# Eight instead of six row blocks under the seven-product scheme, with two of its weight sums made by adding DMAs

## The chip, the cores and the metric

The kernel runs on one core of a Trainium2 chip. A core has five engines with instruction queues of their own: TensorE (PE: matmuls; PEld is its weight load), VectorE (DVE), ScalarE (ACT), GpSimd (POOL) and SyncE (SP), which here only issues DMAs. Sixteen DMA engines move data between the memory (HBM) and the on-chip buffer (SBUF). Matmuls write to PSUM banks. The metric is the device time of one execution, in microseconds; lower is better.

## The reference

A trunk of two layers on 256 tokens of width 2048. Each layer is a token mixer (attention in layer 0, a convolution module in layer 1), an MLP with a squared ReLU, and a gated embedding. All is in float32. The change lies in the MLPs:

```python
def sq_relu_mlp(hn, w1, w2):          # w1: 2048 x 8192, w2: 8192 x 2048
    a = jax.nn.relu(hn @ w1)
    return (a * a) @ w2

for i in range(DEPTH):                # DEPTH = 2
    hn = rmsnorm(h, norm_mix_g[i])
    h = h + (dsa_mixer(...) if i % 2 == 0 else conformer_conv(...))
    h = h + sq_relu_mlp(rmsnorm(h, norm_mlp_g[i]), mlp_w1[i], mlp_w2[i])
    h = h + jax.nn.sigmoid(h @ ple_w_gate[i]) * (p[i] @ ple_w_proj[i])
return rmsnorm(h, final_g)
```

## The kernel before

**Products of float32 numbers.** The 256 tokens are two token blocks of 128 (t). A weight matrix is read in *blocks* of 128 rows by 512 columns (256 KB). TensorE multiplies rounded numbers (float32r), so each operand is split into a rounded high part and the low rest, and each product of blocks is three matmuls: high by high, high by low, low by high. `halves` (lines 295 to 300) splits weights: ScalarE writes `wh` (L298), then VectorE writes `wl` = raw - wh (L299).

**Groups.** Weights are loaded, split and multiplied in groups of up to KG = 3 blocks: one DMA from SP's queue into one of RAWS = 6 `raw` buffers, one ScalarE and one VectorE instruction into one of SPLITS = 4 pairs of buffers `wh`, `wl`. This holds for all weight products of the kernel (`groups` serves `gemm_part` too). In most of the convolution module's first product the `wl` of a group is made by GpSimd.

**pair_gemm.** Each MLP runs in 4 blocks of 2048 hidden columns; a block is two `pair_gemm` calls on w1 and two on w2, so 32 calls in all (*pairs* below). A pair multiplies all 16 row blocks by two column blocks (n = 0, 1) for both t, into four PSUM banks named y, z, v, x. 16 row blocks by 2 by 2 are 64 products. For the first 2 * SP = 6 row blocks a scheme in the manner of Strassen is used: they are SP = 3 couples of an even and an odd row block, and the four weight blocks of a couple are a (even, n=0), b (even, n=1), c (odd, n=0), d (odd, n=1). Seven products with weights a, c, a+b, a+d+b, d, b+d and a+b+d+c take the place of eight (the code makes b+d before it adds it to a). `seven` makes one of the seven for all couples, `plain` the products of the other row blocks. The token side's sums are made once by the class `Sums` (`put`, lines 184 to 199: five small VectorE operations and two splits for a couple, against one split for two ordinary row blocks), and are used by all the pairs that read them.

**Sums of weights.** `add` (L246) adds one `raw` buffer to another on VectorE, 3 blocks at a time: four adds in a pair.

**Partial results.** Some banks are read before they are complete (x1, z1, x2, x3): `taken` reads a bank by ScalarE (L726, on w1) or by VectorE (L760, on w2), and later products write on in that bank, so the first of them waits for the read. Deferred work (`defer`) is written out at the next `step()` calls.

**Order.** The kernel is written in Tile: a scheduler orders each engine's instructions by priority and by its own estimate of time; on the chip every engine then works its queue in that order and waits by semaphores. A load waits until its `raw` buffer is free, a split until its `wh`/`wl` buffers are free, that is, until TensorE has finished the group that had them.

Of the kernel before, what the change touches and what calls it, by code (L numbers as in the profile page):

```python
# [13 lines left out]
ALU = mybir.AluOpType  # L14
# [6 lines left out]
TT = 2  # L21
KT = 16
NB = 512
KG = 3
D_FF = 8192
HD = 128
N_HEADS = 16
# [22 lines left out]
POOL_PW2 = 10  # L50
STATS_LAG = 14
POOL_FROM = 1
SP = 3
HELD = 8
RAWS = 6
SPLITS = 4


@with_exitstack
def encoder(ctx: ExitStack, tc: tile.TileContext, A, inv_freq, out):  # L60
    nc = tc.nc
# [10 lines left out]
    def mm_tile():  # L72
        return ps_mm.tile([P, NB], F32, name="pm", tag="mm")
# [33 lines left out]
    def step():  # L107
        due = [it for it in later if it[0] <= 0]
        later[:] = [it for it in later if it[0] > 0]
        for it in later:  # L110
            it[0] -= 1
        for it in due:
            it[1]()
# [48 lines left out]
    class Sums:  # L162
# [3 lines left out]
        def __init__(self, which, pool):  # L166
            self.main, self.more = [], []
            for p in "hl":
                self.main.append(acts.tile([P, KT, S], F32R, name="x" + p + which, tag="x" + p + which)
                                 .rearrange("p k s -> p (k s)"))  # L170
                self.more.append(pool.tile([P, 3, SP, P], F32R, name="s" + p + which, tag="s" + p + which))
            n = 4 * SP * P
            self.four = [v[:, :n].rearrange("p (m i f) -> p m i f", m=4, i=SP) for v in self.main]
            self.rest = [v[:, n:].rearrange("p (k s) -> p k s", s=S) for v in self.main]
# [37 lines left out]
    def pair_gemm(x, src, taken, first=False):  # L212


        bank = {"x": at_tile(), "y": mm_tile(), "v": mm_tile(), "z": mm_tile()}
        begun, again, left = set(), set(), {"x": 3 * SP, "y": SP, "v": SP, "z": 2 * SP}
        for v in left:
            left[v] += KT - 2 * SP
            left[v] *= 3

        def load(ks, n):
            raw = raw_tile(len(ks))
            nc.sync.dma_start(raw, src[:, ks.start:ks.stop:ks.step, n * NB:(n + 1) * NB])
            return raw

        def product(v, a, b, w, last=False):

            for j, (l, r) in enumerate(((a, w[0]), (a, w[1]), (b, w[0]))):
                left[v] -= 1
                nc.tensor.matmul(bank[v], l, r, start=v not in begun, stop=bool(left[v] == 0 or (last and j == 2)),  # L230
                                 skip_group_check=v in again)
                begun.add(v)
            if left[v] == 0:
                defer(0, lambda: taken(v, bank[v]))
            elif last:
                again.add(v)

        raws = {}

        def raw(name):  # L240
            if name not in raws:
                raws[name] = load(range(name in "cd", 2 * SP, 2), int(name in "bd"))
            return raws[name]

        def add(name, other):
            nc.vector.tensor_tensor(raw(name), raw(name), raw(other), op=ALU.add)  # L246

        def seven(m, v, name, plus=None, part=None):
            step()
            if plus:  # L250
                raw(name), raw(plus)
                add(name, plus)
            w = halves(raw(name))
            for i in range(SP):
                product(v, x.sums(0, m, i), x.sums(1, m, i), (w[0][:, i], w[1][:, i]), part is not None and i == SP - 1)
            if part:
                defer(0, lambda: taken(part, bank[v]))

        def plain(n, ks):
            step()  # L260
            w = halves(load(ks, n))
            for t, v in enumerate("zx" if n else "yv"):
                if t == 1 and len(ks) > 2:
                    step()
                for i, k in enumerate(ks):
                    product(v, x.block(0, k, t), x.block(1, k, t), (w[0][:, i], w[1][:, i]))

        ks = groups(2 * SP, KT - 2 * SP)
        raw("a")
        seven(0, "x", "a", part="x1")  # L270
        seven(5, "y", "c")
        plain(0, ks[0])
        seven(3, "z", "a", "b", part="z1")
        plain(0, ks[1])
        raw("d")
        seven(1, "x", "a", "d", part="x2")
        for r in ks[2:]:
            plain(0, r)
        seven(4, "z", "d")
        seven(2, "x", "b", "d", part="x3")  # L280
        plain_n2 = list(ks)
        seven(6, "v", "a", "c")
        for r in plain_n2:
            plain(1, r)

    def groups(k0, kn):

        n = -(-kn // KG)
        ends = [k0 + kn * i // n for i in range(n + 1)]
        return [range(i, j) for i, j in zip(ends, ends[1:])]  # L290

    def raw_tile(nk, n=NB):
        return wpool.tile([P, KG, NB], F32, name="raw", tag="raw", bufs=RAWS)[:, :nk, :n]

    def halves(r, low=None):

        wh, wl = (wpool.tile([P, KG, NB], F32R, name=v, tag=v, bufs=SPLITS)[:, :r.shape[1], :r.shape[2]] for v in ("wh", "wl"))
        recent[0] = nc.scalar.activation(wh, r, AF.Copy).ins  # L298
        (low or nc.vector).tensor_tensor(wl, r, wh.bitcast(F32), op=ALU.subtract)  # L299
        return wh, wl  # L300
# [539 lines left out]
    with tc.tile_pool(name="cnv", bufs=1) as cnv:  # L840
# [93 lines left out]
        for c, tiles in enumerate(PW_TILES):  # L934
            plan(c)
            n, n0 = len(tiles) * P, tiles[0] * P
# [141 lines left out]
```

## Time and profile before

| | us |
|---|---|
| median of 3 runs | 2275.61 (2275.28 to 2276.20) |
| the profiled execution | 2273.53 |
| its span, first to last instruction | 2271.8 |
| TensorE busy | 2253.1 (99%) |
| VectorE busy | 1783.6 (79%) |
| ScalarE busy | 1298.4 (57%) |
| GpSimd busy | 248.5 (11%) |
| DMA queue of SP | 57% of 16 engines |

The MLPs lie at about 395 to 1050 us and 1480 to 2140 us. One block of an MLP (four pairs) takes 169.73 us, five times alike. Busy shares are means over stages; how long an engine waited, and for whom, stands in the waits.

### The profile page before, as it was taken

Reading aid. Unit: us, or ns where it says so; the run is one execution under the profiler, and the core shown is the slowest. Engines: PE = TensorE matmul, PEld = TensorE weight load, DVE = VectorE, ACT = ScalarE, POOL = GpSimd, SP = SyncE. Lnnn points to the kernel's source line nnn. Section 1 sums busy time; section 2 is a strip of 40 time slices with the busy share of each in tenths; the row PEclk is TensorE's granted clock in tenths of the full one; section 3 lists DMA queues with packets and bytes.
Section 4 is the critical chain, followed back from the end, with each engine's and each line's share of the span. In section 5 each row is a group of like instructions: output and inputs, shape, how many; then the busy total and the mean of one; then the engine's idle time right before and its main releaser. Section 6 shows DMA issues by size and latency. Waiting matters only on the chain.

```text
span 2271.8 us, 27693 instructions
## 1 busy us (share of the span) xinstructions
PE 2253.1 (99%) x10510; PEld 1873.6 (82%) x10510; DVE 1783.6 (79%) x2075; ACT 1298.4 (57%) x1530; POOL 248.5 (11%) x150
## 2 busy tenths in 40 slices
PE   9999999999999999999999999999999999999998
PEld 7888878888888888888898887888888888888886
DVE  5658657888888888887558998788888888888854
ACT  6445546755755755754554644566566566466453
POOL 0112200000000000000038873100000000000001
PEclk9999999999999999999999999999999999999999
DMA  7655445655655655656647552656656656656653
GB/s 267 195 156 172 144 144 161 210 181 190 225 181 190 224 183 191 226 179 201 200 132 222 184 172 83 190 158 211 224 166 209 218 170 209 213 175 217 224 191 102
DMA packets 244869, 425.53 MB, mean 187 GB/s; under 512 B 11636, under 2 KB 57604, under 8 KB 244608
## 3 DMA queue, kind: packets, MB, share of 16 engines
q1 hardware_dynamic: 241872, 419.62, 57.0%
q10 hardware_dynamic: 2864, 4.15, 0.6%
q8 instruction: 82, 1.34, 0.3%
q14 instruction: 51, 0.42, 0.1%
HBM read 421.63 MB, written 2.10 MB: 187 GB/s over the span
## 4 chain that ended last, share of the span: by engine, by line
PE 98%; ACT 0%; DMA 0%; issue 0%; DVE 0%; POOL 0%; SPq 0%; POOLq 0%; DVEq 0%; ACTq 0%
PE pm L230 40%; PE at L230 18%; PE pm L323 11%; PE pm L325 11%; PE pm L324 11%; PE pt L745 1%; PE pm L880 1%; PE pt L404 1%; PE at L591 0%; PE at L638 0%; PE at L668 0%; DMA raw<-in_a_w_in 0%; PE pt L528 0%; PE at L323 0%; PE at L324 0%
## 5 line engine op out<-in xcount | busy, mean ns | idle before, releaser
L298 ACT ACTIVATE wh<-raw 128x1536 fp32r<-128x1536 f32 (+4 forms) x710 | 942.8, 1335 | 757.5 <-PE at L230 255.4
L299 DVE TENSOR_TENSOR wl<-raw,wh 128x1536 fp32r<-128x1536 f32 (+2 forms) x652 | 1033.7, 1598 | 356.8 <-ACT wh L298 354.2
L246 DVE TENSOR_TENSOR raw<-raw 128x1536 f32<-128x1536 f32 x128 | 224.6, 1754 | 19.0 <-DMA raw<-in_mlp_w 18.0
L323 PE MATMUL pm<-wh,xhA 128*128 128x512 f32 (+2 forms) x608 | 234.1, 388 | 1.4 <-ACT xhA L999 1.2
L324 PE MATMUL pm<-wl,xhA 128*128 128x512 f32 (+2 forms) x608 | 233.8, 385 | 0.0
L325 PE MATMUL pm<-wh,xlA 128*128 128x512 f32 (+2 forms) x608 | 231.8, 385 | 0.5 <-DVE xlA L1000 0.4
L324 PE MATMUL pm<-wl,xhB 128*128 128x512 f32 (+1 forms) x576 | 212.4, 369 | 0.0
L325 PE MATMUL pm<-wh,xlB 128*128 128x512 f32 (+1 forms) x576 | 211.5, 368 | 0.0
L323 PE MATMUL pm<-wh,xhB 128*128 128x512 f32 (+1 forms) x576 | 210.7, 369 | 0.4 <-ACT xhB L355 0.4
L230 PE MATMUL pm<-wl,xhB 128*128 128x512 f32 x528 | 206.6, 391 | 0.0
L230 PE MATMUL pm<-wl,xhA 128*128 128x512 f32 x528 | 206.4, 391 | 0.0
L230 PE MATMUL pm<-wh,xlA 128*128 128x512 f32 x528 | 206.2, 391 | 0.0
L230 PE MATMUL pm<-wh,xlB 128*128 128x512 f32 x528 | 206.2, 390 | 0.0
L230 PE MATMUL pm<-wh,xhA 128*128 128x512 f32 x528 | 197.4, 392 | 0.0
L230 PE MATMUL pm<-wh,xhB 128*128 128x512 f32 x528 | 197.2, 391 | 0.0
L909 DVE SCALAR_TENSOR_TENSOR at<-u,wdw,at 128x256 f32<-128x256 f32 x402 | 160.3, 484 | 0.0
L299 POOL TENSOR_TENSOR wl<-raw,wh 128x1536 fp32r<-128x1536 f32 (+3 forms) x58 | 154.4, 2670 | 34.6 <-ACT wh L298 32.6
L323 PEld LDWEIGHTS pm<-wh,xhA 128*128 128x128 f32 x608 | 114.4, 188 | 22.7 <-ACT xhA L999 1.5
L324 PEld LDWEIGHTS pm<-wl,xhA 128*128 128x128 f32 x608 | 114.4, 188 | 21.8 <-DVE wl L299 1.1
L325 PEld LDWEIGHTS pm<-wh,xlA 128*128 128x128 f32 x608 | 114.1, 188 | 22.1 <-DVE xlA L1000 1.4
L323 PEld LDWEIGHTS pm<-wh,xhB 128*128 128x128 f32 x576 | 108.5, 189 | 17.9 <-ACT xhB L355 0.6
L325 PEld LDWEIGHTS pm<-wh,xlB 128*128 128x128 f32 x576 | 108.6, 189 | 17.4 <-issue 0.2
(214 smaller groups left out, 3571.7 us busy)
## 6 DMA issues: line engine op xcount, KB each, us to landing
raw<-in_mlp_w SPq DMA_DIRECT2D x256, 768.0 KB, 6.1
raw<-in_mlp_w SPq DMA_DIRECT2D x128, 512.0 KB, 4.5
raw<-in_a_w_in SPq DMA_DIRECT2D x36, 768.0 KB, 4.3
raw<-in_ple_w_gate SPq DMA_DIRECT2D x32, 768.0 KB, 4.8
raw<-in_b_w_pw SPq DMA_DIRECT2D x48, 384.0 KB, 4.3
raw<-in_a_w_out SPq DMA_DIRECT2D x16, 768.0 KB, 4.5
raw<-in_b_w_pw SPq DMA_DIRECT2D x16, 768.0 KB, 4.4
raw<-in_a_w_in SPq DMA_DIRECT2D x18, 512.0 KB, 3.5
```

Of the source, the lines that this page charges most:

```text
L230: nc.tensor.matmul(bank[v], l, r, start=v not in begun, stop=bool(left[v] == 0 or (last and j == 2)), skip_group_check=v in again)
L246: nc.vector.tensor_tensor(raw(name), raw(name), raw(other), op=ALU.add)
L298: recent[0] = nc.scalar.activation(wh, r, AF.Copy).ins
L299: (low or nc.vector).tensor_tensor(wl, r, wh.bitcast(F32), op=ALU.subtract)
L323: nc.tensor.matmul(pm[t][:, :n], a, wh[:, i], start=k + i == 0, stop=False)
L324: nc.tensor.matmul(pm[t][:, :n], a, wl[:, i], start=False, stop=False)
L325: nc.tensor.matmul(pm[t][:, :n], b, wh[:, i], start=False, stop=k + i == kt - 1)
L404: nc.tensor.transpose(pt[:, k, t, :], h[:, t, (kk + k) * P:(kk + k + 1) * P], ident)
L745: nc.tensor.transpose(pt[:, k, t, :], both[t][:, 2 * j + k, :], ident)
L880: nc.tensor.matmul(acc, d.sets[0][0][:, i, :], u[:, kk, i:i + S], start=i == 0, stop=i == CONV_W - 1)
L909: nc.vector.scalar_tensor_tensor(dst, src, w, z, op0=ALU.mult, op1=ALU.add)
```

## The change

- SP goes from 3 to 4: the scheme covers 8 of 16 row blocks. KG goes from 3 to 2, so a group is two blocks everywhere in the kernel; RAWS goes from 6 to 9 and SPLITS from 4 to 6, which is the same room in SBUF.
- The four couples are two groups (`sets`), so each of the seven products is two splits of two blocks.
- The sums a+b and b+d are no longer made by VectorE from a loaded b: GpSimd issues a DMA that reads b from memory and adds it to the `raw` buffer that holds a (or d). b is never loaded to a buffer of its own, but read twice. The sums with d and c stay on VectorE.
- The order of the products is another, and GpSimd's scratch for DMA descriptors is 2048 instead of 1024.

```diff
-KG = 3
+KG = 2
-SP = 3
+SP = 4
-RAWS = 6
-SPLITS = 4
+RAWS = 9
+SPLITS = 6
...
+        sets = groups(0, SP)
         raws = {}
...
+        def rows(name, q):
+            return range(2 * q.start + (name in "cd"), 2 * q.stop, 2), int(name in "bd")
...
         def add(name, other):
-            nc.vector.tensor_tensor(raw(name), raw(name), raw(other), op=ALU.add)
...
+            for q in sets:
+                r = raw(name, q)
+                if other == "b":
+                    nc.gpsimd.dma_start(r, piece(*rows(other, q)), accum_op=ALU.add)
+                else:
+                    nc.vector.tensor_tensor(r, r, raw(other, q), op=ALU.add)
...
+        def seven(m, v, name, part=None):
+            for q in sets:
+                step()
+                w = halves(raw(name, q))
+                for j, i in enumerate(q):
+                    product(v, x.sums(0, m, i), x.sums(1, m, i), (w[0][:, j], w[1][:, j]), part and i == SP - 1)
...
         ks = groups(2 * SP, KT - 2 * SP)
-        raw("a")
         seven(0, "x", "a", part="x1")
+        add("a", "b")
         seven(5, "y", "c")
-        plain(0, ks[0])
-        seven(3, "z", "a", "b", part="z1")
-        plain(0, ks[1])
-        raw("d")
-        seven(1, "x", "a", "d", part="x2")
-        for r in ks[2:]:
+        for r in ks[:-2]:
             plain(0, r)
+        seven(3, "z", "a", part="z1")
+        add("a", "d")
         seven(4, "z", "d")
-        seven(2, "x", "b", "d", part="x3")
-        plain_n2 = list(ks)
-        seven(6, "v", "a", "c")
-        for r in plain_n2:
+        add("d", "b")
+        seven(1, "x", "a", part="x2")
+        add("a", "c")
+        plain(0, ks[-2])
+        seven(6, "v", "a")
+        seven(2, "x", "d", part="x3")
+        plain(0, ks[-1])
+        for r in ks:
             plain(1, r)
```

What the scheduler makes of it, at three places. On GpSimd, at the two ends of the first MLP, before (the held row belongs to the attention, the memset to the convolution module):

```order
L512 TENSOR_TENSOR work<-held,sin 128x4x64
L511 TENSOR_TENSOR work<-held,nsin 128x4x64
L512 TENSOR_TENSOR work<-held,sin 128x4x64
L652 TENSOR_TENSOR held<-held,sm 128x512 x3
L366 TENSOR_TENSOR rstd<-rp,mhalf 128x2
L842 MEMSET u 128x16x30
```

and after:

```order
L663 TENSOR_TENSOR held<-held,sm 128x512 x3
L256 DMA raw<-in_mlp_w 128x2x512 x2
L377 TENSOR_TENSOR rstd<-rp,mhalf 128x2
L256 DMA raw<-in_mlp_w 128x2x512 x62
L853 MEMSET u 128x16x30
```

GpSimd's queue now holds 64 adding DMAs in an MLP, four in a pair, and nothing else but one small operation.

On VectorE, the first pair on w2 of the first MLP, from the split of a+b on. Before, raw_3903 holds a and its sums, raw_4010 holds d, raw_3922 holds c:

```order
L299 TENSOR_TENSOR wl_3973<-raw_3903,wh_3972 128x1536
L760 TENSOR_TENSOR h_79<-h_79,at_3899 128x512
L246 TENSOR_TENSOR raw_3903<-raw_3903,raw_4010 128x1536
L299 TENSOR_TENSOR wl_3989<-raw_3986,wh_3988 128x1536
L299 TENSOR_TENSOR wl_4014<-raw_3903,wh_4013 128x1536
L299 TENSOR_TENSOR wl_4030<-raw_4027,wh_4029 128x1024
L760 TENSOR_TENSOR h_79<-h_79,pm_3902 128x512
L246 TENSOR_TENSOR raw_3903<-raw_3903,raw_3922 128x1536
```

After, raw_4174 and raw_4186 hold the two groups of a and its sums, raw_4295 and raw_4298 those of d:

```order
L310 TENSOR_TENSOR wl_4276<-raw_4174,wh_4275 128x1024
L258 TENSOR_TENSOR raw_4174<-raw_4174,raw_4295 128x1024
L310 TENSOR_TENSOR wl_4286<-raw_4186,wh_4285 128x1024
L310 TENSOR_TENSOR wl_4303<-raw_4295,wh_4302 128x1024
L310 TENSOR_TENSOR wl_4313<-raw_4298,wh_4312 128x1024
L258 TENSOR_TENSOR raw_4186<-raw_4186,raw_4298 128x1024
L310 TENSOR_TENSOR wl_4325<-raw_4174,wh_4324 128x1024
L367 TENSOR_TENSOR xlB_3393<-pt_4200,xhB_3391 128x512
L367 TENSOR_TENSOR xlB_3393<-pt_4220,xhB_3391 128x512
L310 TENSOR_TENSOR wl_4335<-raw_4186,wh_4334 128x1024
```

The split of d (wl_4303, wl_4313) now stands ahead of that of a+b+d (wl_4325, wl_4335); the adding DMA of b into raw_4295 can start behind wl_4303, that into raw_4298 behind the second add of the piece.

On TensorE, the first pair of the first MLP, after, where z1 is complete (bank pm_3398, the first row) and a+b+d follows in bank at_3395:

```order
L233 MATMUL pm_3398<-wh_3526,xlA_2873 128x512
L233 MATMUL at_3395<-wh_3566,xhA_2871 128x512
L233 MATMUL at_3395<-wl_3567,xhA_2871 128x512
L233 MATMUL at_3395<-wh_3566,xlA_2873 128x512
L233 MATMUL at_3395<-wh_3566,xhA_2871 128x512
L233 MATMUL at_3395<-wl_3567,xhA_2871 128x512
L233 MATMUL at_3395<-wh_3566,xlA_2873 128x512
L233 MATMUL at_3395<-wh_3576,xhA_2871 128x512
L233 MATMUL pm_3396<-wh_3592,xhA_2871 128x512
L233 MATMUL pm_3397<-wh_3592,xhA_2871 128x512
L233 MATMUL at_3395<-wl_3577,xhA_2871 128x512
```

In the code the products of d follow those of a+b in the same bank; in TensorE's queue 14 matmuls stand between the last of a+b and the first of d.

## Rows read from the trace of the kernel before

**Rows 1.** The page: span, and busy time of engines.
```profile
span 2271.8 us, 27693 instructions
PE 2253.1 (99%) x10510; PEld 1873.6 (82%) x10510; DVE 1783.6 (79%) x2075; ACT 1298.4 (57%) x1530; POOL 248.5 (11%) x150
```

**Rows 2.** The page: shares of the chain that ended last, by engine.
```profile
PE 98%; ACT 0%; DMA 0%; issue 0%; DVE 0%; POOL 0%; SPq 0%; POOLq 0%; DVEq 0%; ACTq 0%
```

**Rows 3.** Waits of TensorE, whole span, first and last of nine: total, times, longest.
```profile
PE pt L404 <- issue: 1.5, 1, 1.5
...
PE pm L323 <- ACT xhB L355: 0.4, 1, 0.4
```

**Rows 4.** Timeline of TensorE, 46 matmuls in a row, first and last: start, duration.
```profile
699.70 0.39 PE L230 MATMUL pm<-wl,xhB 128*128 128x512 f32 x1
...
709.90 0.39 PE L230 MATMUL at<-wl,xhB 128*128 128x512 f32 x1
```

**Rows 5.** Busy us by engine in one block (four pairs), clock, DMA share.
```profile
core 0: us, PE busy (x) PEld busy (x) DVE busy (x) ACT busy (x) POOL busy (x), PEclk, DMA share, GB/s
651.81:821.54 169.73, 169.73 (x765) 140.64 (x765) 144.29 (x127) 102.06 (x101) 0.00 (x0) 1.00 0.60 199
```

**Rows 6.** VectorE's groups in that block: busy us, mean ns | idle before.
```profile
L299 DVE TENSOR_TENSOR wl<-raw,wh 128x1536 fp32r<-128x1536 f32 x45 | 78.4, 1755 | 16.8 <-ACT wh L298 16.6
L246 DVE TENSOR_TENSOR raw<-raw 128x1536 f32<-128x1536 f32 x16 | 28.1, 1754 | 2.0 <-DMA raw<-in_mlp_w 1.8
L299 DVE TENSOR_TENSOR wl<-raw,wh 128x1024 fp32r<-128x1024 f32 x16 | 19.5, 1221 | 4.5 <-ACT wh L298 4.4
L356 DVE TENSOR_TENSOR xlB<-pt,xhB 128x512 fp32r<-128x512 f32 x5 | 3.2, 684 | 0.0
L356 DVE TENSOR_TENSOR slB<-work,shB 128x384 fp32r<-128x384 f32 x3 | 1.7, 554 | 0.0
L194 DVE TENSOR_TENSOR work<-work 128x128 f32<-128x128 f32 x3 | 0.9, 284 | 0.0
L193 DVE TENSOR_SCALAR work<-work 128x128 f32<-128x128 f32 x3 | 0.7, 219 | 0.0
```

**Rows 7.** ScalarE's groups in that block.
```profile
L298 ACT ACTIVATE wh<-raw 128x1536 fp32r<-128x1536 f32 x44 | 65.4, 1489 | 48.3 <-PE at L230 27.5 <-DVE raw L246 8.7 <-PE pm L230 7.9
L298 ACT ACTIVATE wh<-raw 128x1024 fp32r<-128x1024 f32 x16 | 16.9, 1058 | 15.8 <-PE pm L230 8.3 <-PE at L230 5.1 <-issue 2.4
L726 ACT ACTIVATE held<-at 128x512 f32<-128x512 f32 x6 | 3.6, 596 | 2.0 <-PE at L230 2.0
L355 ACT ACTIVATE shB<-work 128x384 fp32r<-128x384 f32 x3 | 1.5, 509 | 0.0
```

**Rows 8.** Waits in that block: total us, times, longest.
```profile
ACT wh L298 <- PE at L230: 32.6, 21, 3.5
...
ACT wh L298 <- PE pm L230: 16.2, 14, 2.8
ACT wh L298 <- DVE raw L246: 8.7, 3, 4.3
ACT wh L298 <- DMA raw<-in_mlp_w: 3.4, 3, 1.6
```

**Rows 9.** DMA issues of the MLPs: count, KB each, median us to landing.
```profile
raw<-in_mlp_w SPq DMA_DIRECT2D x256, 768.0 KB, 6.1
raw<-in_mlp_w SPq DMA_DIRECT2D x128, 512.0 KB, 4.5
```

**Rows 10.** GpSimd's weight splits, by form: busy us, mean ns.
```profile
L299 POOL TENSOR_TENSOR wl<-raw,wh 128x1536 fp32r<-128x1536 f32 x26 | 91.1, 3507 | 15.9 <-ACT wh L298 15.9
L299 POOL TENSOR_TENSOR wl<-raw,wh 128x1024 fp32r<-128x1024 f32 x14 | 33.7, 2407 | 5.5 <-ACT wh L298 3.7 <-DMA raw<-in_b_w_pw 1.3
```

**Rows 11.** Busy us by engine in 100 us of the convolution module.
```profile
1200.00:1300.00 100.00, 100.00 (x472) 83.19 (x471) 89.82 (x230) 57.41 (x89) 86.18 (x28) 1.00 0.63 198
```

More of the change, by code (lines that the diff above doesn't have):

```diff
@@ L219, in pair_gemm, with piece @@
             left[v] *= 3
+        def piece(ks, n):
+            return src[:, ks.start:ks.stop:ks.step, n * NB:(n + 1) * NB]
         def load(ks, n):
             raw = raw_tile(len(ks))
-            nc.sync.dma_start(raw, src[:, ks.start:ks.stop:ks.step, n * NB:(n + 1) * NB])
+            nc.sync.dma_start(raw, piece(ks, n))
             return raw
@@ L236, in product, with raw @@
                 again.add(v)
+        sets = groups(0, SP)
         raws = {}
[L240 to L243, printed above, removed]
-        def add(name, other):
-            nc.vector.tensor_tensor(raw(name), raw(name), raw(other), op=ALU.add)
[L248 to L255, printed above, removed]
+        def rows(name, q):
+            return range(2 * q.start + (name in "cd"), 2 * q.stop, 2), int(name in "bd")
+        def raw(name, q):
+            if (name, q) not in raws:
+                raws[name, q] = load(*rows(name, q))
+            return raws[name, q]
+        def add(name, other):
+            for q in sets:
[10 more added lines that the diff above has]
+                    product(v, x.sums(0, m, i), x.sums(1, m, i), (w[0][:, j], w[1][:, j]), part and i == SP - 1)
             if part:
@@ L1062 @@
     from concourse.bass_utils import run_bass_kernel_spmd
-    nc = bacc.Bacc("TRN2", target_bir_lowering=False, num_devices=1, dynamic_dma_scratch_size=1024)
+    nc = bacc.Bacc("TRN2", target_bir_lowering=False, num_devices=1, dynamic_dma_scratch_size=2048)
     arrays, aps = {}, {}
```

## The prediction

> **What bounds the kernel now.** I read the page's busy times first, then the chain that ended last, then TensorE's own waits, then one block of an MLP by engine and by group. TensorE is busy for 2253.1 of 2271.8 us [rows 1], and the chain is TensorE for 98% of the span [rows 2]. Busy matmuls can still be waiting ones, so the reader should see that TensorE's waits are nine rows that run from 1.5 us down to 0.4 us, all outside the MLPs [rows 3], and that 46 matmuls in a row start at one step: (709.90 - 699.70) / 45 = 0.2267 us [rows 4]. One block of an MLP is four pairs of 183 matmuls, 732 x 0.2267 = 165.9 us, and 32 transposes; it takes 169.73 us with TensorE busy all the time at granted clock 1.00, 2.4 GHz [rows 5]. So the MLPs are a queue of matmuls without holes, and a matmul less is worth its step as long as everything else keeps up. What has to keep up: VectorE is busy 144.29 of 169.73 us, 85%, the DMA engines 60% [rows 5]. The splits run ahead: ScalarE's longest waits are for TensorE to give back a wh buffer, 32.6 + 16.2 us in the block [rows 8]. This lead is what a late weight sum would eat first.
>
> **The change, part by part.** *Matmuls.* Six row blocks need 21 products, ten ordinary ones 40: 61 products, 183 matmuls a pair. Eight and eight need 28 + 32 = 60 products, 180 matmuls. Three a pair, 32 pairs: 96 x 0.2267 = 21.8 us [rows 4], all on the path. A block should go to 169.73 - 2.72 = 167.0 us.
>
> *VectorE's work in a block.* Splits before: 44 of three blocks at 1.755 us and 16 of two at 1.221, together 96.8 us. After: 22 groups of two in each of four pairs, 88 x 1.221 = 107.4 us. Adds before: 16 x 1.754 = 28.1 us; after 16 of two blocks, which I take at the split's 1.221 since at three blocks the two operations cost the same, 19.5 us. One more couple of sums in a block: 0.219 + 4 x 0.284 us, and splits of 0.684 + 0.554 in place of one of 0.684, so 1.9 us [rows 6]. Sum +4.0 us: 148.3 of 167.0 us, 89%. This lies beside the matmuls and costs nothing; the cover is the 18.7 us left, 4.7 us a pair. Had the two sums with b stayed on VectorE, 16 adds more (19.5 us) would have made 167.8 us, over the block. ScalarE: 88 splits at 1.058 against 44 at 1.489 and 16 at 1.058, +10.6 us [rows 7] on 102.06: 67%, hidden.
>
> *Groups of two elsewhere.* The same matmuls. Where GpSimd makes the wl, a product of 16 row blocks costs it 8 x 2.407 = 19.3 us against 4 x 3.507 + 2 x 2.407 = 18.8 [rows 10]; it was busy 86.18% there [rows 11], so 88%, hidden under TensorE's 100%. Without that cover it would be 0.4 us a product. I take 0.
>
> *The adding DMAs.* Their length is the one thing that the trace does not show. Call D the time from the moment GpSimd may issue one to the sum's arrival. GpSimd's queue holds nothing else in an MLP but one small operation, so nothing is stuck behind its waits. Behind a late sum are ScalarE's and VectorE's queues: the split of the sum stands in both, and whatever follows waits with it. How late D may be follows from queue order. A group of the scheme is six matmuls, 1.36 us; an ordinary group is twelve, 2.72 us; the six wh buffers let a split begin when TensorE ends the group six earlier; a split takes 1.06 us on ScalarE and 1.22 on VectorE [rows 6, 7]. Start the clock when the first split of a may begin. TensorE still has five ordinary groups (13.6 us) in front of a, so it ends the first group of a at 14.96 us, and then the split of a+b may begin. The split of a is done at 2.3 us, so D up to 12.7 us costs nothing; TensorE itself reaches a+b only at 24.5 us, so it would stand still from D = 19.9 on. The sum b+d is the tight one. The two splits of d are done at about 20.9 and 22.1 us (VectorE's order in the second fence of its place: split, add, split, split, split, add), the second add at 23.3. TensorE ends d at 32.6 and reaches b+d at 38.1. In between ScalarE could split b+d at 32.6 and 33.7, so D up to 11.7 and 10.4 us costs nothing. Beyond, the lead shrinks, and TensorE waits when the second group of b+d comes later than 37.2 us (39.44, less 2.28 for its split): D = 13.9. In pairs on w1 it is earlier, since ScalarE reads x2 only behind that split, and TensorE needs that read at 38.1: 38.1 - 1.06 - 0.51 - 0.60 = 35.9, D = 12.6 [rows 7]. Mean 13.2 us.
>
> The bounds of D: a plain load of 512 KB lands in 4.5 us, in traffic as it is [rows 9]; below that there is no reason to go. An adding DMA has two operands to read, one from memory and one from the buffer, so two loads on end, 9.0 us, is the dear price for one; and if the second group's DMA has to wait for the first wholly, four loads on end less the 2.4 us that it is issued later: 15.6 us. I take 9.0, since the DMA engines were only 60% busy [rows 5] and can work on both. It is under 10.4, so the price is 0; at 15.6 it would be 2.4 us a pair.
>
> The Trainium skill, DMA: Bandwidth & Descriptors, section Rules for kernel authors, says that an accumulating DMA reads its destination and writes it later. No trace here shows one; by that page the dear price is the right one for a single DMA, and the sum stays as it is.
>
> *Reads before completion.* In the code the products of d follow those of a+b in bank z, and would wait for z1's read, 0.60 us and more of ScalarE [rows 7]. In TensorE's queue 14 matmuls stand between, 3.2 us, so 0; without them it would be 0.6 us and more a pair.
>
> *The sum.* Against the profiled execution: 2273.53 (span 2271.8 and 1.73 around it) - 21.8 = 2251.8 us. The median of the runs shown is 2.1 us above that execution, so 2253.8 us; I say **2254**.
>
> **The rivals.** *b+d comes too late (slower).* Place: the second split of b+d. Price: D - 13.2 us a pair, 32 pairs. It has eaten the gain at D = 13.9 us, and at 15.6 it gives 2254 + 32 x 2.4 = 2331 us. For it: two DMAs close behind each other, a busy DMA system, GpSimd's issue time unknown. Against it: 13.2 us is almost three plain loads, and ScalarE's waits for TensorE show a real lead.
>
> *The DMA engines become the bound.* A block keeps them busy for 0.60 x 169.73 = 102 us for 128 weight blocks, 0.80 us each [rows 5]. After, 112 plain blocks are 89.1 us, and of 167.0 us 77.9 are left for 32 adding ones: 2.43 us each, 3.1 times a plain one. At twice a plain one they are 84% busy and nothing happens; at four times a block needs 191 us, 24 us more in each of 8 blocks: 2254 + 192 = 2446 us. The Trainium skill, DMA: Bandwidth & Descriptors, section Issuing engines are not separate DMA queues, says that DMAs from all issuing engines run on the same 16 engines and interleave, which speaks against this change: the added reads are not a free second path. Here nearly all bytes are on SP's queue, so no row shows two queues in competition; by that rule the time is still 2254 up to the factor of 3.1.
>
> *Part of the gain is lost.* D between 10.4 and 13.2 us leaves ScalarE and VectorE idle in most pairs; VectorE has 4.7 us a pair to give. With two sums late by 2 to 3 us each in a pair it gives them all, and a hole of 0.1 to 0.6 us a pair comes to TensorE: 2257 to 2273 us.
>
> That the change doesn't do what it says can be put aside: the built queue of TensorE holds 5760 matmuls in the pairs against 5856.
>
> **How the numbers follow.** Full gain, within a few us: 0.60 (2250 to 2258 us). Part of it: 0.16, of which 0.12 still faster than by 0.2% (2258 to 2271) and 0.04 within. b+d late: 0.18, of which 0.02 lands within 0.2%. DMA engines the bound: 0.06. About 0.2% (4.6 us, 2271.1 to 2280.2) is what a measurement of this kernel can tell from no change. So faster 0.72, same 0.06, slower 0.22. The range begins at 2250, the full gain and a little from the smaller first loads, and reaches to 2290, b+d late by up to 1.1 us a pair; what is left out are the dearer ends of the two slow cases, about 0.18.
>
> **What would show it.** A block at 167.0 us with TensorE busy all through, VectorE near 148 us, the DMA share at 0.75 to 0.85, and landings of the adding DMAs at 6 to 10 us: right. Waits of a matmul for a wh or wl of b+d, or of ScalarE's split for the adding DMA over 4.7 us a pair: the first rival. DMA share near 1.0 and plain loads that land late: the second. A block of 169.7 us without holes in TensorE would make the count of matmuls wrong; VectorE's 1.221 us grown while GpSimd issues would make its budget wrong.

## The result, and the profile after

The changed kernel takes 2257.89 us (median of 4 runs, 2256.54 to 2258.46) against 2275.9 us of the kernel before: a ratio of 0.9923, interval 0.991 to 0.9935. Five more runs of it, beside nine new ones of the kernel before, gave 2258.21 us against 2275.1 (0.9928, interval 0.9916 to 0.9941). The forecast was 2254 us in a range of 2250 to 2290. Faster was right and the time lies in the range, but of the 21.8 us of matmuls taken away only 17 to 18 arrive. The question of this part is where the other 4 went, and whether the reasons for the rest were the right ones.

Page of the kernel after, span and busy times [rows 1], then its two large DMA queues (q1 is SP's, q0 holds GpSimd's adding DMAs: packets, MB, share of 16 engines):

```profile
span 2256.7 us, 29464 instructions
PE 2234.9 (99%) x10414; PEld 1857.5 (82%) x10414; DVE 1811.2 (80%) x2412; ACT 1395.5 (62%) x1856; POOL 403.4 (18%) x297
...
q1 hardware_dynamic: 228016, 386.08, 51.6%
q0 software_dynamic: 34816, 67.12, 17.8%
```

One block of an MLP, the same as [rows 5], with the same columns, and VectorE's and ScalarE's main groups in it, as [rows 6, 7]:

```profile
653.05:820.12 167.07, 167.07 (x753) 138.18 (x753) 146.47 (x161) 112.11 (x132) 19.36 (x16) 1.00 0.81 227
```

```profile
L310 DVE TENSOR_TENSOR wl<-raw,wh 128x1024 fp32r<-128x1024 f32 x88 | 105.1, 1220 | 19.3 <-ACT wh L309 17.8
L258 DVE TENSOR_TENSOR raw<-raw 128x1024 f32<-128x1024 f32 x17 | 20.7, 1218 | 0.1
...
L309 ACT ACTIVATE wh<-raw 128x1024 fp32r<-128x1024 f32 x88 | 91.7, 1058 | 50.1 <-PE at L233 23.4 <-PE pm L233 19.4 <-DVE raw L258 6.0
```

The block is 167.07 us long and TensorE is busy for all of it at clock 1.00: the forecast block of 167.0. VectorE has 146.47 us of work in it (forecast 148.3), the DMA engines are busy for 0.81 (forecast 0.75 to 0.85), and ScalarE still waits for TensorE to give back its buffers, 23.4 + 19.4 us [rows 8]. No split waits for an adding DMA. GpSimd's queue in one pair of that block shows why (start, duration, idle time before and its releaser; two DMAs of a+b, two of b+d), and below it the landings (KB each, median us from issue):

```profile
667.70 1.21 POOL L256 DMA_DIRECT2D raw<-in_mlp_w  x1 [19.16 <-DVE wl L310]
669.43 1.20 POOL L256 DMA_DIRECT2D raw<-in_mlp_w  x1 [0.52 <-DVE wl L310]
685.21 1.20 POOL L256 DMA_DIRECT2D raw<-in_mlp_w  x1 [14.58 <-DVE wl L310]
687.48 1.21 POOL L256 DMA_DIRECT2D raw<-in_mlp_w  x1 [1.07 <-DVE wl L310]
```

```profile
raw<-in_mlp_w SPq DMA_DIRECT2D x448, 512.0 KB, 5.5
raw<-in_mlp_w POOLq DMA_DIRECT2D x128, 512.0 KB, 6.5
```

An adding DMA goes out as soon as VectorE has split the group, and lands 6.5 us later. That is D, taken as 9.0 in bounds of 4.5 to 15.6.

**Where the 4 us went** is seen when the span is cut at the first and the last matmul of each MLP. Five stages of the kernel before, then of the kernel after (columns of [rows 5]):

```profile
0.00:379.10 379.10, 374.72 (x1807) 311.10 (x1807) 242.51 (x367) 202.97 (x312) 52.00 (x66) 1.00 0.56 178
379.10:1061.84 682.74, 682.74 (x3090) 565.51 (x3088) 578.85 (x516) 412.52 (x417) 2.64 (x2) 1.00 0.61 199
1061.84:1479.08 417.24, 412.88 (x2086) 349.44 (x2085) 325.46 (x625) 220.59 (x322) 180.08 (x73) 1.00 0.54 167
1479.08:2161.71 682.63, 682.63 (x3089) 565.32 (x3087) 578.51 (x514) 411.95 (x418) 2.15 (x1) 1.00 0.61 200
2161.71:2271.80 110.09, 100.17 (x446) 82.22 (x444) 58.29 (x56) 50.37 (x63) 11.67 (x8) 0.98 0.44 143
```

```profile
0.00:382.65 382.65, 376.14 (x1806) 312.17 (x1807) 246.32 (x403) 208.93 (x344) 54.79 (x68) 0.99 0.59 179
382.65:1054.03 671.38, 671.38 (x3036) 555.30 (x3035) 589.42 (x651) 453.47 (x541) 76.23 (x64) 1.00 0.81 227
1054.03:1474.05 420.02, 415.37 (x2090) 352.10 (x2089) 326.65 (x647) 227.90 (x360) 185.65 (x94) 0.99 0.55 167
1474.05:2145.45 671.40, 671.40 (x3036) 555.27 (x3035) 589.42 (x651) 453.70 (x541) 75.72 (x63) 1.00 0.81 228
2145.45:2256.70 111.25, 100.63 (x450) 82.69 (x448) 59.42 (x64) 51.48 (x70) 11.01 (x8) 0.97 0.41 133
```

The MLPs give 682.74 - 671.38 = 11.36 and 682.63 - 671.40 = 11.23 us, 22.6 together, and the three other stages cost 3.55 + 2.78 + 1.16 = 7.5 us. Not all of this is gain and loss. In the kernel before, 32 transposes of h (the residual, turned on TensorE for the products that follow) stand between the first and the last matmul of each MLP. In the kernel after there are 28, and four stand right behind the last matmul (start, duration):

```profile
1054.27 0.60 PE L415 MATMUL pt<-ident,h 128*128 128x128 f32 x4
1054.62 0.48 PE L334 MATMUL pm<-wh,xhA 128*128 128x512 f32 x1
```

From 1054.03 to 1054.62 us are 0.59 us where a step between two matmuls is 0.23, and the step behind is 0.32: these four cost 0.45 us, which the cut counts as a gain of the MLP and as a loss of the stage behind it. So the MLPs give 22.6 - 0.9 = 21.7 us, the forecast gain, and the loss outside is 6.6 us in these two profiles. This profile of the kernel before lies 2.1 us under its median; by medians the loss is what is missing of 21.8, about 4 us.

It is not spread evenly. TensorE's instructions ahead of the first MLP are as many before and after (1806), so they can be compared one by one. The 151st starts at 37.70 us before and at 40.20 and 41.11 us in two profiles of the kernel after; the 1501st at 312.63, 315.35 and 316.27. So 2.5 to 3.4 us are lost in the first 40 us, where the DMA engines are full from 10 to 30 us, and next to nothing in the 270 us behind. Between the MLPs nearly all of the loss, some 2 us, comes at 1358 to 1394 us, at the end of the convolution, where VectorE is busy for all of 1350 to 1370 us. There TensorE has two waits that the kernel before does not have (before, it waits 1.2 us there for ScalarE; total, times, longest):

```profile
PE pt L934 <- DVE u L966: 1.4, 1, 1.4
PE pt L934 <- DVE u L920: 1.0, 1, 1.0
```

### The profile page after: what moved, and what is told of

Its sections match the earlier page's. It is cut to its first block, busy times and chain, and to the rows that moved or that the text cites. A ratio compares the mean times of both kernels' runs of the same rounds, so it can differ in the third digit from the quotient of the medians.

```text
span 2256.7 us, 29464 instructions
## 1 busy us (share of the span) xinstructions
PE 2234.9 (99%) x10414; PEld 1857.5 (82%) x10414; DVE 1811.2 (80%) x2412; ACT 1395.5 (62%) x1856; POOL 403.4 (18%) x297
## 3 DMA queue, kind: packets, MB, share of 16 engines
q1 hardware_dynamic: 228016, 386.08, 51.6%
q0 software_dynamic: 34816, 67.12, 17.8%
## 4 chain that ended last, share of the span: by engine, by line
PE 95%; DVE 2%; DMA 2%; ACT 1%; issue 1%; POOL 0%; SPq 0%; POOLq 0%; ACTq 0%; DVEq 0%
PE pm L233 39%; PE at L233 19%; PE pm L336 10%; PE pm L334 10%; PE pm L335 10%; PE pt L756 1%; DVE at L920 1%; DMA raw<-in_a_w_in 1%; PE pt L415 1%; PE at L602 0%; PE at L649 0%; PE at L679 0%; DMA work<-in_b_w_dw 0%; PE pt L539 0%; PE at L334 0%
## 5 line engine op out<-in xcount | busy, mean ns | idle before, releaser
L309 ACT ACTIVATE wh<-raw 128x1024 fp32r<-128x1024 f32 (+2 forms) x1008 | 1036.1, 1040 | 665.6 <-PE pm L336 227.5
L310 DVE TENSOR_TENSOR wl<-raw,wh 128x1024 fp32r<-128x1024 f32 (+1 forms) x931 | 1118.6, 1221 | 327.0 <-ACT wh L309 304.8
L256 POOL DMA_DIRECT2D raw<-in_mlp_w x128 | 155.0, 1211 | 1200.5 <-DVE wl L310 1163.5
L233 PE MATMUL pm<-wl,xhB 128*128 128x512 f32 x448 | 175.9, 393 | 0.0
L233 PE MATMUL pm<-wl,xhA 128*128 128x512 f32 x448 | 175.9, 393 | 0.0
L233 PE MATMUL pm<-wh,xlA 128*128 128x512 f32 x448 | 174.6, 391 | 0.0
L233 PE MATMUL pm<-wh,xlB 128*128 128x512 f32 x448 | 174.6, 391 | 0.0
L233 PE MATMUL pm<-wh,xhA 128*128 128x512 f32 x448 | 170.9, 392 | 0.0
L233 PE MATMUL pm<-wh,xhB 128*128 128x512 f32 x448 | 170.9, 392 | 0.0
L310 POOL TENSOR_TENSOR wl<-raw,wh 128x1024 fp32r<-128x1024 f32 (+1 forms) x77 | 158.4, 2074 | 29.2 <-ACT wh L309 28.2
L258 DVE TENSOR_TENSOR raw<-raw 128x1024 f32<-128x1024 f32 x128 | 155.9, 1218 | 1.0
L334 PEld LDWEIGHTS pm<-wh,xhA 128*128 128x128 f32 x608 | 115.2, 190 | 22.6 <-ACT xhA L369 0.6
L233 PE MATMUL at<-wh,xlB 128*128 128x512 f32 x320 | 125.2, 391 | 0.0
```

The costliest lines, as they stand in the source:

```text
L256: nc.gpsimd.dma_start(r, piece(*rows(other, q)), accum_op=ALU.add)
L258: nc.vector.tensor_tensor(r, r, raw(other, q), op=ALU.add)
L334: nc.tensor.matmul(pm[t][:, :n], a, wh[:, i], start=k + i == 0, stop=False)
```

## The experiments

Each run is the changed kernel with the edit shown, unless said otherwise. The numbers of the kernel before next to it are from the same chip.

### Only the sums on VectorE again

```diff
-                    nc.gpsimd.dma_start(r, piece(*rows(other, q)), accum_op=ALU.add)
+                    nc.vector.tensor_tensor(r, r, load(*rows(other, q)), op=ALU.add)
```

> The changed kernel with a+b and b+d made by VectorE: b is loaded by SP to a raw buffer each time (twice in a pair, as the adding DMA reads it twice) and added there. In the changed kernel VectorE is busy for 146.47 of 167.07 us of a block; 16 adds of 1.218 us are 19.5 more: 166.0 us, 99%. Theory (VectorE has no room for the two sums, and the adding DMA is what pays for the eighth row block): TensorE gets holes, a block takes 168 to 172 us, 2266 to 2298 us in all. Rival (the sums could as well stay on VectorE): 2258 us, a block of 167.1 us.

Measured: 2280.06 us (2279.7 to 2282.06), 1.0023 of before (1.0013 to 1.0032). All of the gain is gone and 4.5 us more. The first MLP of this run, and what TensorE waited for in the whole run (total, times, longest):

```profile
381.21:1064.73 683.52, 676.39 (x3037) 554.04 (x3035) 652.24 (x713) 447.22 (x541) 1.20 (x2) 1.00 0.67 223
...
PE pm L233 <- DVE wl L310: 7.7, 18, 0.9
PE at L233 <- DVE wl L310: 6.3, 8, 1.1
```

VectorE is busy for 652.24 of 683.52 us, 95%, and TensorE's waits name its splits. (This run also loads b to buffers of its own; ScalarE's splits wait for a load for only 5.2 us of that MLP.) So the same number of matmuls as in the kernel after takes 12.1 us longer in each MLP. The adding DMAs are not a side matter: without them eight row blocks gain nothing. VectorE is the bound well before its busy time reaches the block: 652.24 / 4 = 163.1 us in a block of 170.9.

### Only the groups, buffers and adding DMAs, with six row blocks

```diff
-SP = 4
+SP = 3
```

> The changed kernel with six row blocks under the scheme (SP = 3), all else as changed: groups of two (a set of couples is then one and two blocks), adding DMAs, the new order of products. 96 matmuls of 0.2267 us more than the changed kernel. Theory (the MLPs give the whole 21.8 us, and what is missing is lost outside them, by the groups of two in the other stages): the MLPs go back to 682.7 us each, the stages outside stay at their 914 us of the changed kernel: 2257.9 + 21.8 = 2279.7 us, 3.8 above the kernel before. Rival (the loss outside is chance, of the granted clock and of landings in single executions): 2276 us, as before. Rival (the pairs themselves run less well with adding DMAs, and eight row blocks hide it): a block of four pairs over 169.73 us.

Measured: 2277.50 us (2276.97 to 2279.06, 10 runs), 1.001 of before (1.0 to 1.002), between the two numbers expected. The stages:

```profile
0.00:381.32 381.32, 376.56 (x1807) 312.44 (x1807) 244.30 (x398) 206.95 (x342) 54.50 (x68) 1.00 0.58 177
381.32:1063.98 682.66, 682.66 (x3088) 565.11 (x3087) 545.90 (x660) 431.15 (x562) 67.00 (x64) 1.00 0.76 218
1063.98:1483.05 419.07, 414.27 (x2086) 350.69 (x2085) 325.76 (x641) 225.90 (x357) 186.74 (x94) 1.00 0.54 165
1483.05:2165.72 682.67, 682.67 (x3089) 565.10 (x3088) 545.89 (x660) 431.15 (x562) 66.52 (x63) 1.00 0.77 220
2165.72:2275.70 109.98, 100.15 (x446) 82.22 (x444) 58.75 (x63) 50.86 (x69) 11.04 (x8) 0.97 0.42 134
```

With six row blocks the MLPs are at 682.66 and 682.67 us, the kernel before to within 0.1 us: groups of two, the new order and adding DMAs cost nothing there and give nothing. So the whole gain of the MLPs is the eighth and seventh row block, and the 2.0 us that this run is slower than before are outside them: 2.2 us before the first MLP and 1.8 between the two in this profile. They are the two places of the kernel after: the 151st instruction of TensorE starts at 40.07 us here, and both waits for u are there. Of the loss of about 4 us outside, 2 come with groups of two and their buffers, and the other 2 come only with the fourth couple (381.32 to 382.65, 419.07 to 420.02, 109.98 to 111.25, less the transposes that the cut moves).

### Two places outside the MLPs mended

In the first profile of the kernel after, the granted clock fell near the start. Two runs on one chip, the kernel as it is and one with two edits: more transposes ahead of the first work, and the transposes of the convolution's taps, for which TensorE had waited twice 0.7 us, three steps later.

```diff
-WARM0 = 18
+WARM0 = 26
...
-        defer(1, turn)
+        defer(4, turn)
```

> The changed kernel itself again, to be compared on one chip with the next one. Both theories: 2258 us. If the granted clock at 10 to 20 us is 1.00 in this profile, its fall in the first profile was of that execution and not of the kernel.

> The changed kernel with two edits outside the MLPs: 26 instead of 18 transposes ahead of the first real work on TensorE, and the transposes of the convolution's taps three steps later behind their DMAs. Theory (part of what the groups of two lost outside the MLPs is the fall of the clock at the start, 2.4 us, and the two waits for the taps, 1.3 us): 3 to 4 us faster than the changed kernel, 2254 to 2255 us. Rival (the loss lies in the many small differences of the splits by two, and the two places only move): within 1 us of the changed kernel, 2257 to 2259 us.

Measured: 2258.21 us (2257.96 to 2259.61) unchanged, 2258.09 us (2257.53 to 2259.25) with the edits; the rival's number. From 5 to 20 us in steps of 5 us, the first profile of the kernel after, then its second profile, then the kernel with the edits:

```profile
5.00:10.00 5.00, 1.60 (x13) 1.11 (x12) 1.72 (x5) 2.93 (x8) 0.00 (x0) 0.83 0.88 289
10.00:15.00 5.00, 4.79 (x14) 3.38 (x15) 3.21 (x5) 3.61 (x7) 0.00 (x0) 0.50 1.04 385
15.00:20.00 5.00, 5.00 (x16) 3.88 (x16) 3.40 (x5) 3.22 (x6) 0.00 (x0) 0.64 1.05 387
```

```profile
5.00:10.00 5.00, 2.74 (x13) 1.91 (x12) 1.57 (x5) 3.01 (x8) 0.00 (x0) 1.00 0.85 282
10.00:15.00 5.00, 4.95 (x18) 3.55 (x19) 3.60 (x6) 3.75 (x7) 0.00 (x0) 1.00 1.05 396
15.00:20.00 5.00, 5.00 (x28) 4.22 (x27) 3.84 (x7) 4.17 (x9) 0.00 (x0) 1.00 1.05 388
```

```profile
10.00:15.00 5.00, 3.19 (x10) 1.94 (x9) 2.71 (x4) 3.23 (x5) 0.00 (x0) 0.68 1.03 392
```

The third number from the right is the clock: it is 0.50 (1.2 GHz) at 10 to 15 us in the first profile, 1.00 in the second, 0.68 with the edits. The first MLP begins at 382.65, 382.6 and 383.5 us all the same. In this stretch the DMA engines are at 1.03 to 1.05, full: the weights set the pace there, and a matmul that runs faster only waits longer (at 30 to 35 us TensorE is busy for 4.80 of 5 us in the first profile and for 3.12 in the second). So the fall of the clock at the start, which looked like 2.4 us in the first profile, costs nothing, and neither do the taps: with the edits their waits are gone and the time is the same. The two waits for u were not tried, and no version that beats the changed kernel came out of this.

### b+d held up

GpSimd is given small work of its own ahead of the first adding DMA of b+d in each pair: a one-column copy that reads the wl of d, so that it starts when the DMA could, and a power on a number of columns. Nothing of the computation is left out. Four doses: the copy alone, without the power, and 12, 28 and 60 columns. `keep` holds these instructions in the order of the code.

```diff
+                    if name in SLOW and q.start == 0:
+                        keep(nc.gpsimd.tensor_copy(junk[:, 2 * DELAY:], lows[name][:, 0, :1].bitcast(F32)))
+                        keep(nc.gpsimd.tensor_tensor(junk[:, :DELAY], ones, ones, op=ALU.pow))
-                    nc.gpsimd.dma_start(r, piece(*rows(other, q)), accum_op=ALU.add)
+                    keep(nc.gpsimd.dma_start(r, piece(*rows(other, q)), accum_op=ALU.add))
```

> The changed kernel with GpSimd held up before the first adding DMA of each b+d by one slow operation on 28 columns of a scratch tile, about 4 us by the trace's durations for one and two columns of it. Today such a sum is there 6.5 us after its issue begins, so D becomes about 11 us. Theory (the prediction's queue arithmetic: free up to 10.4 to 11.7 us, TensorE waits only from 12.6 us in pairs on w1 and 13.9 on w2): ScalarE waits for the DMA by 1 us here and there, TensorE for nothing, 2258 us within 2. Rival (the lead is smaller than worked out): holes on TensorE already here, 1 us a pair or 32 us.

> As the run with 28 columns, but 60 of them, about 8.2 us: D is about 15.2 us. The order of the groups on TensorE is the same, the fine order of ScalarE and VectorE is planned anew around the later sum. Theory: TensorE waits 15.2 - 12.6 us in 16 pairs and 15.2 - 13.9 in the other 16, 62 us in all: 2320 us. Rival (what is queued behind a late sum is re-ordered or the lead takes it all): 2258 us. Rival (the lead is smaller): 2350 us and more.

> The changed kernel with a smaller delay ahead of the first adding DMA of b+d: the one-column copy alone (3.9 us in the mean in the earlier run, scattered from 0.2 to 13.7), so about 11.8 us to the landing. Nothing of the computation is left out. Theory (a threshold near 13 us, below it the lead of the splits hides the delay): most pairs lose nothing, those with a long copy lose some us: 2258 to 2300 us. Rival (no threshold: each us of delay costs about 0.6 us, the slope between the delays of 9.3 and 14.6 us): 4 us a pair, about 2386 us.

> b+d held up by the one-column copy and a pow on 12 columns. In the earlier runs the copy took 1.04 us in three pairs of four and 12 to 13.7 us in the fourth, so the sum takes about 12.4 us in three pairs and 22 us and more in the fourth. Nothing of the computation is left out. Theory (TensorE waits only from 12.6 us in w1 pairs and 13.9 us in w2 pairs): the three pairs cost next to nothing (under 1 us), the fourth 2 to 3 us more than with the copy alone: 2365 to 2400 us. Rival (no point from which it decides; the three pairs go evenly from 0.3 us at 8.5 us to 7 us at 15.7 us): 3.5 us more in each of 24 pairs besides, about 2460 us.

Measured: copy alone 2352.37 us (1.0346 of before, 1.0332 to 1.036); 12 columns 2345.02 (1.0305, 1.0289 to 1.032); 28 columns 2493.37 (1.0958, 1.0937 to 1.098); 60 columns 2597.39 (1.1416, 1.1393 to 1.1438). The delays of the first two runs were longer than meant (9.3 and 14.6 us in the mean), so the times that they were expected to give can't be held against them as they stand; and with the copy alone and with 12 columns the times lie between the two theories or under both. The means hide why. The copy alone, shortest, median and longest in ns:

```profile
L263 POOL COPY junk<-wl x32: 181/1042/13692, 395.8 to 2205.5; 128x1 f32<-128x1 f32 x32
```

In most pairs it takes 1.04 us, but in the second w1 pair of each block 12 to 13.7 us. So a run has more than one dose, and they can be read pair by pair. In the run with the copy alone, the short w2 pairs follow each other in 40.72 and 40.60 us (kernel after: 40.40 and 40.33): next to no loss. Nearly all of the loss is in one pair of four. That pair in the first block (copy from 439.45 to 453.13 us; windows of 10 and 5 us), and the matmul that ended TensorE's wait:

```profile
440.00:450.00 10.00, 10.00 (x48) 8.24 (x48) 10.00 (x17) 6.77 (x12) 10.00 (x1) 1.00 0.21 61
450.00:455.00 5.00, 5.00 (x24) 4.09 (x23) 3.09 (x5) 0.39 (x1) 5.00 (x3) 1.00 0.96 307
455.00:460.00 5.00, 1.27 (x6) 0.70 (x4) 0.00 (x0) 0.00 (x0) 0.51 (x1) 1.00 0.95 196
460.00:465.00 5.00, 0.00 (x0) 0.00 (x0) 1.22 (x1) 1.65 (x2) 0.00 (x0) 0.57 0.62 113
465.00:470.00 5.00, 3.44 (x7) 2.45 (x8) 4.36 (x5) 5.00 (x8) 0.00 (x0) 0.50 0.71 212
```

```profile
466.41 0.80 PE L238 MATMUL at<-wh,xhA 128*128 128x512 f32 x1 [10.14 <-ACT held L747]
```

VectorE and ScalarE run dry behind the late sum (0.00 busy at 455 to 460 us), TensorE has matmuls up to 456.3, and then stands still for 10.14 us until ScalarE has read x2: in this w1 pair it is that read, behind the split of b+d, that comes last, as the prediction had it. That holds in two of the eight long pairs of this run. In the other six, such as that of 620.80 us, x2 was read long before (629.40 us), and TensorE waits for the splits of b+d themselves, 5.33 and 0.57 us. While it stands the clock falls, 1.00 at 455 to 460 us and 0.57 at 460 to 465; TensorE comes back at 0.50, and a matmul takes 0.63 us instead of 0.39 for some 4 us more.

The prediction counted from queue order that TensorE waits when the second sum is later than 12.6 us in w1 pairs and 13.9 in w2 pairs, counted from 2.4 us after the first DMA may start. Pairs of three runs, each with the start of the copy, the start of the second split of b+d, and TensorE's waits there:

| run, pair | copy, split (us) | D of the second sum | limit | wait forecast | wait measured |
|---|---|---|---|---|---|
| 12 columns, w1 | 576.40, 591.83 | 13.0 | 12.6 | 0.4 | 0.0 |
| 12 columns, w2 | 535.49, 551.91 | 14.0 | 13.9 | 0.1 | 0.03 |
| 28 columns, w2 | 545.89, 565.62 | 17.3 | 13.9 | 3.4 | 3.0 |
| copy alone, w1 | 620.80, 642.84 | 19.6 | 12.6 | 7.0 | 5.9 |
| copy alone, w1 | 439.45, 464.41 | 22.6 | 12.6 | 10.0 | 10.1 |

These five lie close to the forecast; not all do. Over all 96 pairs of these three runs the forecast wait and the measured one differ by up to 2.6 us, by over 1 us in 27 of the 57 pairs beyond D = 13; summed by run, 65, 54 and 172 us were forecast and 59, 50 and 160 measured. With 60 columns TensorE waits up to 4 us less than forecast. The limit itself stands out: no pair with D up to 12.5 us waits for more than 0.04 us, those from 12.5 to 14.5 wait for 0 to 0.8 us, and every pair from 15.5 on waits for 1.25 us or more. That w1 pairs have the earlier limit is not seen: five of them from 12.9 to 13.5 us wait for nothing, and the one at 14.3 us for 0.12.

The split of the second row of the table, and that pair's window:

```profile
547.84 1.06 ACT L320 ACTIVATE wh<-raw 128x1024 fp32r<-128x1024 f32 x1 [2.55 <-DMA raw<-in_mlp_w]
551.91 2.01 ACT L320 ACTIVATE wh<-raw 128x1024 fp32r<-128x1024 f32 x2 [3.01 <-DMA raw<-in_mlp_w]
```

```profile
535.49:576.40 40.91, 40.88 (x179) 33.34 (x178) 34.60 (x34) 22.96 (x23) 9.17 (x6) 1.00 0.82 231
```

ScalarE does wait for the DMA there (2.55 and 3.01 us), and TensorE does not: 40.88 of 40.91 us busy. So there is a point from which a late b+d decides, and it lies where queue order puts it, to within 2 us. Beyond it the price is more than the wait: the copy alone costs 2352.37 - 2258.21 = 94 us, of which 4.9 lie ahead of the first MLP (it begins at 387.5 us) and 89 in the two. Of these, waits of TensorE for the sums are 34.8 + 20.1 + 3.3 = 58, and the other 31 are longer busy time (687.52 and 686.01 us for 671.4 in each), at a mean clock of 0.97 and 0.98.

### a+b held up

The same ahead of a+b, with 28, 60 and 80 columns (SLOW names a instead of d).

> The changed kernel with GpSimd held up ahead of the first adding DMA of a+b in each pair, by the same two small operations (a one-column copy, a pow on 28 columns; about 9 us together in the run that held up b+d, so about 17 us from the moment it may issue to the landing). Nothing of the computation is left out. Theory (each sum has its own latest time, set by where TensorE's queue has it): a+b may come 19.9 us late before TensorE stands still, so the time is that of the changed kernel and a little for the longest copies: 2258 to 2300 us, and TensorE's waits for the split of a+b are few. Rival (a late sum costs the same wherever it stands, because ScalarE's and VectorE's queues stand still behind it): as with b+d, 7.4 us a pair, about 2490 us.

> As the run that held up a+b, with the pow on 60 columns. There the delay was 5.0 us a pair (the one-column copy took only 0.18 us ahead of a+b), so about 11.6 us from the moment the DMA may be issued to the sum; here the pow takes 10 to 11 us, so about 17.5 us. Nothing of the computation is left out. Theory (the queue order of the prediction: TensorE stands still from 19.9 us on, though ScalarE's and VectorE's lead is eaten from 12.7 on): the MLPs stay within 1 us a pair of the changed kernel's 671.4 us, time 2260 to 2295 us. Rival (the same delay costs a+b what it costs b+d, where 17.3 us in the mean cost 7.4 us a pair): about 2490 us.

> The same with 80 columns, 13.5 to 14.5 us of delay, so about 21 us to the sum, 1 us beyond the point from which TensorE should stand still for a+b. Theory: 1 us of waiting a pair and with it a fall of the clock, 1 to 4 us a pair: 2290 to 2390 us, and TensorE's waits name the split of a+b. Rival 1 (a+b behaves as b+d does): over 2550 us. Rival 2 (a+b has still more room): 2260 to 2275 us.

Measured: 28 columns 2263.47 us (0.9951 of before, 0.9936 to 0.9966), 60 columns 2449.09 (1.0766, 1.0742 to 1.079), 80 columns 2493.76 (one run). Ahead of a+b the copy takes 0.18 us in most pairs, so the doses are plain: about 5, 10 and 13 us.

At 28 columns (about 11.3 us to the sum) the MLPs take 671.6 and 672.4 us: the delay is free, as "up to 12.7 us costs nothing" said, and the 5.3 us that this run is slower than the kernel after are mostly outside the MLPs (the first begins at 386.5 us; the runs with b+d held up, 385.7 to 387.5). I don't know what in the edit does that.

At 60 columns the MLPs are at 764.4 and 767.6 us: the time is far nearer to the rival's 2490 than to my 2260 to 2295, and my theory falls. (At 80 columns they are at 786.7 and 788.5 us, and none of the three numbers fits.) One pair, in windows of 5 us (copy at 567.79, splits of a+b at 584.85 and 588.32 us), and TensorE's longest waits:

```profile
580.00:585.00 5.00, 5.00 (x24) 4.14 (x23) 0.00 (x0) 0.67 (x2) 0.29 (x1) 1.00 1.02 207
585.00:590.00 5.00, 4.90 (x21) 3.50 (x19) 3.04 (x3) 2.59 (x3) 0.00 (x0) 1.00 0.57 107
590.00:595.00 5.00, 1.94 (x6) 1.05 (x6) 5.00 (x5) 3.06 (x4) 1.51 (x2) 1.00 0.20 25
595.00:600.00 5.00, 4.77 (x21) 3.95 (x22) 4.93 (x6) 3.22 (x6) 0.92 (x1) 1.00 1.09 184
600.00:605.00 5.00, 5.00 (x24) 4.14 (x23) 4.95 (x5) 4.95 (x6) 0.00 (x0) 1.00 1.02 363
```

```profile
PE at L238 <- DVE wl L321: 27.8, 13, 2.8
```

The first sum is 17.1 us late and TensorE is still busy up to 589 us: it does not wait for that split (0.04 us). For the second one, read 20.5 us after the copy began and so about at the limit itself, it waits 0.76 us. But VectorE had nothing to do for five us (0.00), and from 590 us on it is at 4.93 to 5.00 of 5, while TensorE waits 2.46 us for a split of a+b+d; in some w1 pairs, as that of 996.77 us, this is the only wait. VectorE needs 36.6 of a pair's 41.8 us; idle time forced on it beyond some 5 us a pair can't be made up, wherever TensorE itself stands. That is how I read it, and it is not shown; a run that gives VectorE more room with the same delay wasn't made. What is shown is that a+b is free at 11.3 us and costs (764.4 - 671.4) / 16 = 5.8 us a pair at 17.

## Why the prediction was right, and where not

- **Matmuls, 21.8 us on the path: right.** The MLPs give 21.7 us, with the four transposes put back in each, and the run with six row blocks shows that nothing else of the change moves them.
- **VectorE's budget: right.** 146.47 us in a block for 148.3; the add of two blocks at 1.218 us for the 1.221 taken. That the two sums with b on VectorE would have cost the gain is shown by the run that put them there. The size was too high, 163.1 for 167.8 us, since instructions that follow without a gap overlap (starts some 1.14 us apart for 1.22 us of duration); the bound is met below 100%.
- **Groups of two elsewhere, taken as 0: the step that failed.** It was costed for GpSimd's splits in the convolution alone. The loss is about 4 us by medians: 2 with the groups and their buffers, and 2 with the fourth couple, for which the sum has no term outside the MLPs. This is the whole difference between 2254 and 2258. Most of it lies in the first 40 us, where the weights set the pace, and at the end of the convolution, where VectorE does. Why groups of two are slower there stays open: the two places that were mended gave nothing.
- **D = 9.0 us: mis-sized without effect.** It is 6.5 us, nearer to a plain load (5.5 us in this traffic) than to two on end.
- **The limit of b+d, 12.6 and 13.9 us: right to within 2 us**, but not the difference between w1 and w2: x2's read comes last in few pairs, and w1 pairs wait no earlier. The rival that b+d comes too late was thus a real one, 6 us away; and its price of 1 us for each us beyond was too low (89 us in the MLPs for 58 of waits), since the clock falls during the wait.
- **The limit of a+b, 19.9 us: wrong**, but not a term of the sum. "D up to 12.7 us costs nothing" held at 11.3; that only the lead shrinks between 12.7 and 19.9 did not hold at 17, since TensorE then waits at a+b+d, which the count for a+b left out.
- **DMA engines: right.** Share 0.81 for 0.75 to 0.85 forecast. 0.81 x 167.07 = 135.3 us, less 112 plain blocks if they still take 0.80 us, leaves 32 adding ones at 1.44 us, 1.8 times a plain one; the queue rows of the page give 2.0 times (17.8% of the span for 67.12 MB, 51.6% for 386.08 MB). The bound was at 3.1 times. The Trainium skill, DMA: Bandwidth & Descriptors, section Rules for kernel authors, says that an accumulating DMA reads its destination too; 1.8 to 2.0 times the engine time agrees with that, the landing of 6.5 us does not show it.
- **Reads before completion: right.** TensorE has no wait in the block.

## What to carry to other kernels

Before a sum is moved to a DMA, count in queue order how late it may be, once for the engine at the end and once for each engine that runs dry behind it: the count for TensorE's queue put the limit of b+d to within 2 us, and failed for a+b, where, as I read it, VectorE at 88% could no longer catch up. A constant that holds for the whole kernel (a group's size, a pool) has to be costed in every stage, since about 4 of 22 us were lost where nothing was to change. When a span is cut at an instruction, count what stands on either side of the cut: 0.9 us here was work that had only moved across it. And a clock or a wait that stands out in one profile is only worth mending where TensorE sets the pace: where the DMA engines were full, full clock and half clock gave the same time.

## What the runs showed of the hardware

**GpSimd's copy beside VectorE.** A copy of one column took 0.18 us, or 1.04, or up to 13.7. With 1.04 us it ended just behind the VectorE instruction that ran when it came (495.56 to 496.61 us, the instruction up to 496.56), though the next one had already begun. In the longest case it began at 439.45 and ended at 453.13 us, and VectorE worked from before it up to 453.09 without a gap, on additions and subtractions of two operands in SBUF but for two operations of 0.2 us. GpSimd's adding DMAs, issued beside the same kind of work, took 1.19 to 1.36 us each in the kernel after, never more. The Trainium skill, SBUF — State Buffer, section Who interferes with whom, says that a VectorE instruction with two SBUF inputs contends with a GpSimd instruction that reads SBUF, and that what they contend for is an exclusive lock. The trace agrees that the copy is held: in most pairs for one instruction, in eight for a whole row of them. What decides between the two is not shown.

**The clock after a wait.** TensorE stood still from 456.28 to 466.41 us. The granted clock was 1.00 at 455 to 460 us, 0.57 at 460 to 465 and 0.50 (1.2 GHz) at 465 to 470, and a late sum so cost about half as much again as its wait (89 us in the MLPs for 58).

**The adding DMA.** 512 KB: 1.21 us of GpSimd to issue, 6.5 us to landing (5.8 to 8.8), 1.8 to 2.0 times the engine time of a plain load. Two issued back to back, as behind the delays, land 2.5 to 4.1 us apart in most pairs (547.74 and 551.80 us, 461.72 and 464.32 us), though the second is issued within 1 us of the first.
